# Low parts of the weights kept from the first half, and a selection operand shared by the groups, in a hybrid convolution and state-space layer

## The chip, the cores and the metric

The kernel runs on one core of a Trainium2 chip. The metric is the device time of one execution in microseconds. Three timed executions of the kernel before took 1994.49 to 1999.12 us, with a median of 1996.78 us. One more execution was recorded by the hardware profiler, and all rows shown here come from that one. The engines are called TensorE (PE in the rows), VectorE (DVE), ScalarE (ACT), GpSimd (POOL) and SyncE (SP, which issues most of the DMAs).

## The reference

One layer over 1024 positions and 1024 channels in float32, cut to its core:

```python
h = layer_norm(x, ln_in_g, ln_in_b)
u = h @ w_in[l]     # GLU | ssm z | ssm x,B,C | ssm dt | gate_a | gate_b
y_a = conformer_branch(u_glu, ...)  # GLU, 31-tap causal conv, LN, silu, @ w_conv_out
y_b = ssd_branch(z, xbc, dt_raw, ...)  # 4-tap conv, chunked SSD, group RMS norm, @ w_ssm_out
mix = (sigmoid(gate_a) * y_a + sigmoid(gate_b) * y_b) @ w_o[l]
h = layer_norm(DN_ALPHA * h + mix, ln1_g[l], ln1_b[l])
h = layer_norm(DN_ALPHA * h + conv_ffn(h, ...), ln2_g[l], ln2_b[l])
```

The SSD part has 32 heads of 64 channels in 4 groups of 8 heads, a state of 128, and chunks of 128 positions. Within a chunk, with a the decay rates of the chunk's positions:

```python
a_cs = jnp.cumsum(a, axis=-1)
seg = a_cs[..., :, None] - a_cs[..., None, :]
decay = jnp.where(causal, jnp.exp(jnp.where(causal, seg, 0.0)), 0.0)
cb = jnp.einsum("bclgn,bcsgn->bcgls", cc, bc)
y_diag = jnp.einsum("bcgrls,bcsgrp->bclgrp", cb[:, :, :, None] * decay, xs)
```

A scan over the chunks carries the state from one to the next.

## The kernel before

**Halves.** The 1024 positions are worked on as two halves of 512 (hh = 0 and 1 in the names, so `w_gt0_7` belongs to the first and `w_gt1_7` to the second). Each half goes through the input layer norm, `mixers`, `combine` and `out_proj`; the FFN follows for both. The projection weights of the mixers, the combination and the output are fetched from DRAM again in the second half.

**Weights.** Every product of float32 operands is made of three matmuls (`mm3`, L187 to L189) over a high and a low part. `weights` (L158) loads a tile of 128 x 1024 (512 KB) on SP into one of three staging buffers `st`, ScalarE casts it to the high part in `w[:, 0]` (L163), and VectorE subtracts that from `st` to give the low part in `w[:, 1]` (L164). There are three `w` buffers as well. `project` runs 24 matmuls for one tile, each with 512 columns. In the rest of the text these 512-column matmuls are called filler matmuls where they stand between the small products of the SSD part.

**Mixers.** For each of four groups: columns of the input projection and the four-tap convolution (`conv4`, L429), the GLU (L451, L452), the SSD chunks (`ssd_group`), z's gates (`z_gate`, L492) and the 31-tap convolution on VectorE (`conv31`, L474), whose result is stored to `c_scr` (L483). In a chunk, x and B are transposed (L520, L523), C and B are multiplied (L524) and masked to `cbm` (L546), and GpSimd forms `au` (L526), 8 copies of the decay selection `seg_mv`, one for each head of the group. Two matmuls (L535) of `seg_st` with `au` give the segment sums, which relu and exp turn into `m` (L543, L544). `xs` and `xsd` (L548, L553) are x times the step sizes; `bt` (L557) is B transposed, copied by ScalarE. L563 reads the state, L567 makes the chunk's contribution to it from `bt` and `xsd`, and L569 or L571 and L574 update it on VectorE. L577 gives y.

**Group norm.** The squares of a group's four tiles are added up on GpSimd (L602). `normed`, which runs later, sums them over the channels (L607), takes root and reciprocal (L612, L613), writes them to `r_scr` (L615), reads them back to all partitions into `ss` (L616), scales the tiles (L619) and splits them into `yT` (L203, L204).

**Combine.** Gate projections `gb`, the second half of the SSD output projection `sp` (which reads `yT` of the groups 2 and 3) and `co`, the convolution's output projection. In between stands the layer norm of the convolution: its eight tiles come back from `c_scr` (L696), GpSimd adds them up (L703, L705), and a matmul gives the mean (L707). That part has the scheduling priority `tc.high_priority(offset=900)`.

**Order.** The order of instructions on each engine isn't written by hand: a scheduler places them by a simulated timeline and by priorities, `offset=4000` for weights, and `offset=-1500` for the 31-tap convolution. Each engine then works through its list in order, and SP's list of DMAs too.

## Time and profile before

| | |
|---|---|
| median of three timed executions | 1996.78 us (1994.49 to 1999.12) |
| profiled execution, own time | 1997.45 us |
| its span, first to last instruction | 1995.7 us |
| granted TensorE clock, mean | 0.997 |
| VectorE, 31-tap convolution (L474) | 480 instructions, 385.2 us busy |
| GpSimd, `au` (L526) | 32 instructions, 79.8 us busy |
| GpSimd, squares (L602) | 24 instructions, 41.1 us busy |
| read and written in DRAM | 229.44 MB and 50.09 MB |

Busy shares say how much of the span an engine worked. A row of waits names an engine and a line that stood still, what it stood still for, and how long. A row of the timeline begins with the start and the duration in us; behind it, in brackets, stands how long the engine was idle before. A row of a line gives minimum, median and maximum of its durations in ns. A row of the DMA table gives the queue, the size and the median time from issue to landing in us.

### The profile page before, as it was taken

The numbers are of one execution on the slowest core, as the hardware profiler recorded it, in microseconds if no ns is written. First come the engines' busy times: TensorE is split into PE (matmuls) and PEld (weight loads), VectorE is DVE, ScalarE is ACT, GpSimd is POOL, SyncE is SP. The second block draws the span as 40 slices with busy tenths as digits, with TensorE's granted clock in tenths as the row PEclk, the third lists the DMA queues.
The fourth block names the chain that finished last, engine by engine and source line by source line (L and its number), as shares of the span: only waits on it lengthen the run. The fifth ranks groups of instructions, "written<-read, shape, count | busy, mean of one in ns | idle before, by whom it ended". The sixth has DMA issues, their size and how long they took to land.

```text
span 1995.7 us, 24843 instructions
## 1 busy us (share of the span) xinstructions
PE 1947.5 (98%) x9240; PEld 1592.9 (80%) x9240; DVE 1701.1 (85%) x2230; ACT 1052.9 (53%) x1483; POOL 237.4 (12%) x201
## 2 busy tenths in 40 slices
PE   7999999999999999999999999999999999999998
PEld 6887777877788887788777878887878888888886
DVE  7899999989565879999999967578998888778768
ACT  5566767454453266667654646256554544553442
POOL 1112121101400001111210132001000000011000
PEclk9999999999999999999999999999999999999999
DMA  6324232523544642324243354476443232268573
GB/s 218 111 65 121 73 117 79 164 81 115 175 127 155 240 140 77 102 84 117 80 132 116 100 185 127 132 279 241 170 148 116 101 113 104 102 215 272 181 248 111
DMA packets 99241, 281.15 MB, mean 141 GB/s; under 512 B 11728, under 2 KB 11760, under 8 KB 99120
## 3 DMA queue, kind: packets, MB, share of 16 engines
q1 hardware_dynamic: 87840, 244.68, 36.9%
q0 software_dynamic: 8976, 30.69, 5.1%
q10 hardware_dynamic: 2304, 4.20, 0.6%
q8 instruction: 72, 1.18, 0.2%
q14 instruction: 49, 0.40, 0.1%
HBM read 229.44 MB, written 50.09 MB: 140 GB/s over the span
## 4 chain that ended last, share of the span: by engine, by line
PE 64%; DVE 27%; issue 5%; DMA 2%; ACT 1%; POOL 1%; SPq 0%; DVEq 0%; POOLq 0%; ACTq 0%
PE acc L189 16%; PE acc L187 16%; PE acc L188 16%; DVE c L474 11%; PE sm L187 3%; PE sm L189 3%; PE sm L188 3%; DVE xbc L429 2%; DVE w_c L164 1%; PE acc L411 1%; DVE w_z L164 1%; DMA ss<-r_scr 1%; DVE m L558 1%; DVE xbc L619 1%; POOL mean L705 1%
## 5 line engine op out<-in xcount | busy, mean ns | idle before, releaser
L474 DVE SCALAR_TENSOR_TENSOR c<-v,pc,c 128x512 f32<-128x512 f32 x480 | 385.2, 832 | 5.5 <-ACT c L463 4.3
L187 PE MATMUL acc<-hT,w_c 128*128 128x512 f32 x352 | 141.6, 402 | 0.0
L189 PE MATMUL acc<-hT,w_c 128*128 128x512 f32 x352 | 138.5, 394 | 0.0
L188 PE MATMUL acc<-hT,w_c 128*128 128x512 f32 x352 | 137.9, 392 | 0.0
L526 POOL TENSOR_TENSOR au<-seg_mv,head_of 128x1024 fp32r<-128x1024 f32 x32 | 79.8, 2494 | 374.0 <-PE sm L535 373.9
L429 DVE SCALAR_TENSOR_TENSOR xbc<-u,pc,xbc 128x512 f32<-128x512 f32 x144 | 112.3, 794 | 0.5 <-ACT xbc L427 0.4
L987 DVE SCALAR_TENSOR_TENSOR fo<-u,pc,fo 128x1024 f32<-128x1024 f32 x88 | 111.4, 1286 | 0.4 <-ACT fo L983 0.4
L187 PE MATMUL acc<-h1s,w_s 128*128 128x512 f32 x264 | 103.5, 392 | 2.3 <-ACT u L971 2.3
L188 PE MATMUL acc<-hT,w_z 128*128 128x512 f32 x256 | 103.7, 405 | 0.0
L189 PE MATMUL acc<-h1s,w_s 128*128 128x512 f32 x264 | 103.0, 390 | 0.0
L188 PE MATMUL acc<-h1s,w_s 128*128 128x512 f32 x264 | 102.7, 389 | 0.0
L187 PE MATMUL acc<-hT,w_z 128*128 128x512 f32 x256 | 101.7, 397 | 0.0
L189 PE MATMUL acc<-hT,w_z 128*128 128x512 f32 x256 | 101.6, 397 | 0.0
L1126 ACT CAST w_dn<-dr 128x1024 fp32r<-128x1024 f32 (+1 forms) x73 | 61.0, 843 | 69.8 <-DVE dr L1056 33.3
L1127 DVE TENSOR_TENSOR w_dn<-dr,w_dn 128x1024 fp32r<-128x1024 f32 (+1 forms) x73 | 70.1, 968 | 13.5 <-ACT w_dn L1126 13.2
L188 PEld LDWEIGHTS acc<-hT,w_c 128*128 128x128 f32 x352 | 66.1, 188 | 15.7 <-issue 2.4
L187 PEld LDWEIGHTS acc<-hT,w_c 128*128 128x128 f32 x352 | 66.2, 188 | 15.3 <-issue 2.4
L189 PEld LDWEIGHTS acc<-hT,w_c 128*128 128x128 f32 x352 | 66.1, 188 | 14.5 <-issue 0.8
L163 ACT CAST w_c<-st_c 128x1024 fp32r<-128x1024 f32 x48 | 50.2, 1045 | 51.6 <-PE acc L189 32.5
L187 PE MATMUL sm<-h1b,w_s 128*128 128x512 f32 x176 | 69.1, 393 | 0.0
L188 PE MATMUL sm<-h1b,w_s 128*128 128x512 f32 x176 | 69.0, 392 | 0.0
L189 PE MATMUL sm<-h1b,w_s 128*128 128x512 f32 x176 | 69.0, 392 | 0.0
(372 smaller groups left out, 5708.3 us busy)
## 6 DMA issues: line engine op xcount, KB each, us to landing
st_c<-wcol SPq DMA_DIRECT2D x50, 512.0 KB, 3.5
st_z<-wz SPq DMA_DIRECT2D x32, 512.0 KB, 3.4
st_wo<-wo SPq DMA_DIRECT2D x24, 512.0 KB, 4.1
ra<-wup SPq DMA_DIRECT2D x22, 512.0 KB, 3.5
rb<-wup SPq DMA_DIRECT2D x22, 512.0 KB, 3.5
t_scr<-fo POOLq DMA_DIRECT2D x22, 512.0 KB, 3.4
dr<-t_scr SPq DMA_DIRECT2D x44, 256.0 KB, 3.8
dr<-wdown SPq DMA_DIRECT2D x38, 256.0 KB, 4.5
```

The costliest lines, as they stand in the source:

```text
L163: A.copy(w[:, 0, :], st)
L164: (eng or V).tensor_tensor(out=w[:, 1, :], in0=st, in1=w[:, 0, :].bitcast(F32), op=ALU.subtract)
L187: TE.matmul(ps, wa(0), xa(0), start=start, stop=False, skip_group_check=more)
L188: TE.matmul(ps, wa(0), xa(1), start=False, stop=False, skip_group_check=more)
L189: TE.matmul(ps, wa(1), xa(0), start=False, stop=stop, skip_group_check=more)
L411: TE.matmul(ps[:, ts], w[:, i, k * P : (k + 1) * P], hT[:, j, k, ts], start=n == 0 and k == 0, stop=n == 2 and k == KD - 1,)
L429: V.scalar_tensor_tensor(out=o, in0=u[:, k : k + HALF], scalar=pc[:, wc + k : wc + k + 1], in1=o, op0=ALU.mult, op1=ALU.add,)
L474: V.scalar_tensor_tensor(out=accs[i], in0=v[:, k : k + HALF], scalar=pc[:, wc + k : wc + k + 1], in1=accs[i], op0=ALU.mult, op1=ALU.add,)
L526: G.tensor_tensor(out=au, in0=seg_mv[:, c, :].unsqueeze(1).to_broadcast([P, 8, P]), in1=head_of[:, g, :].unsqueeze(2).to_broadcast([P, 8, P]),
L987: V.scalar_tensor_tensor(out=o, in0=u[:, k : k + T], scalar=pc[:, wc + k : wc + k + 1], in1=o, op0=ALU.mult, op1=ALU.add,)
L1126: A.copy(w[:, 0, cs], src)
L1127: V.tensor_tensor(out=w[:, 1, cs], in0=src, in1=w[:, 0, cs].bitcast(F32), op=ALU.subtract)
```

## The change

**Low parts.** In the first half `weights` stores each tile's low part to DRAM after the subtraction (96 tiles, 512 KB each, on SP). In the second half the same tile's low part is loaded into `w[:, 1]` on SP, and the subtraction is left out. Names that begin with `wo` (the weights of `out_proj`) are excluded, so the renaming in the last hunk changes a name only.

**Selection operand.** `au` is formed with all heads' lanes (`head_all`) and no longer depends on the group: GpSimd forms it for group 0 and stores it (8 times), and for the groups 1 to 3 it is loaded back on GpSimd's queue (24 times, 512 KB). The group enters through the other operand: ScalarE multiplies `seg_st` by the group's lanes into `sg` (128 x 128).

**Smaller edits.** The copy to `bt` stands right behind B's transposition. The squares of a group are added on VectorE. z's projections and their activations go in pairs. The convolution's layer norm has the priority 300 in place of 900. Two small reductions at the start form the lanes.

```diff
@@ -1,3 +1,4 @@
+import re
 from contextlib import ExitStack
 
 import concourse.bass as bass
@@ -112,6 +113,12 @@
         axis=AX.X,
         op=ALU.add,
     )
+    lanes = statep.tile([P, 16], F32, name="lanes")
+    head_all, group_of = lanes[:, :8], lanes[:, 8:12]
+    V.tensor_reduce(
+        out=head_all, in_=head_of.rearrange("p g h -> p h g"), axis=AX.X, op=ALU.add
+    )
+    V.tensor_reduce(out=group_of, in_=head_of, axis=AX.X, op=ALU.add)
     kind = const.tile([P, 4], F32, name="kind")
     V.tensor_reduce(
         out=kind, in_=ident.rearrange("p (g k h) -> p k g h", k=4, h=8), axis=AX.XY, op=ALU.add
@@ -152,18 +159,34 @@
     c_scr = [dram.tile([8, P, HALF], F32, name=f"c_scr{i}") for i in range(2)]
     g_scr = [dram.tile([8, P, HALF], F32, name=f"g_scr{i}") for i in range(2)]
     e_scr = [dram.tile([P, HALF], F32, name=f"e_scr{i}") for i in range(2)]
+    au_scr = [
+        [dram.tile([P, 8 * P], F32R, name=f"au_scr{i}_{c}") for c in range(4)] for i in range(2)
+    ]
     r_scr = [dram.tile([GROUPS, HALF], F32, name=f"r_scr{i}") for i in range(2)]
     y_scr = [dram.tile([8, P, HALF], F32, name=f"y_scr{i}") for i in range(2)]
 
+    low_scr = {}
+
     def weights(src, name, pl=None, eng=None, bufs=None):
+        half = re.match(r"([a-z]+)([012])_(.*)$", name)
+        if name.startswith("wo"):
+            half = None
+        key = half and (half.group(1), half.group(3))
         with tc.high_priority(offset=4000):
             st = wst.tile([P, D], F32, tag="st", name=f"st_{name}")
             SY.dma_start(st, src)
             w = (pl or wsp).tile([P, 2, D], F32R, tag="w", bufs=bufs, name=f"w_{name}")
+            if half and half.group(2) != "0" and key in low_scr:
+                SY.dma_start(w[:, 1, :].bitcast(F32), low_scr[key])
+                A.copy(w[:, 0, :], st)
+                return w
             A.copy(w[:, 0, :], st)
             (eng or V).tensor_tensor(
                 out=w[:, 1, :], in0=st, in1=w[:, 0, :].bitcast(F32), op=ALU.subtract
             )
+        if half and half.group(2) == "0":
+            low_scr[key] = dram.tile([P, D], F32, name=f"low_{name}")
+            SY.dma_start(low_scr[key], w[:, 1, :].bitcast(F32))
         return w
 
     def weights_side_by_side(src, name):
@@ -485,12 +508,14 @@
     def z_gate(pl, hh, hT, g):
 
         zs = []
-        for i in range(4):
-            ps = bank(1)
-            project(ps, weights(wz[4 * g + i], f"z{hh}_{g}_{i}"), hT)
-            z = pl.tile([P, HALF], F32, tag="zs", bufs=5, name=f"zs{hh}_{g}_{i}")
-            A.activation(out=z, in_=ps, func=AF.Silu)
-            zs.append(z)
+        for i in range(0, 4, 2):
+            pss = [bank(1) for _ in range(2)]
+            for k, ps in enumerate(pss):
+                project(ps, weights(wz[4 * g + i + k], f"z{hh}_{g}_{i + k}"), hT)
+            for k, ps in enumerate(pss):
+                z = pl.tile([P, HALF], F32, tag="zs", bufs=5, name=f"zs{hh}_{g}_{i + k}")
+                A.activation(out=z, in_=ps, func=AF.Silu)
+                zs.append(z)
         return zs
 
     def ssd_group(pl, hh, g, xT, BT, CT, gate):
@@ -521,20 +546,28 @@
             pb = bank(0)
             if not last:
                 TE.transpose(pb[:, :P], BT[:, cs], ident)
+                bt = pl.tile([P, P], F32, tag="bt", name=f"bt{nm}")
+                A.copy(bt, pb[:, :P])
             TE.matmul(pb[:, P : 2 * P], BT[:, cs], CT[:, cs], start=True, stop=True)
             au = pl.tile([P, 8, P], F32R, tag="au", name=f"au{nm}")
-            G.tensor_tensor(
-                out=au,
-                in0=seg_mv[:, c, :].unsqueeze(1).to_broadcast([P, 8, P]),
-                in1=head_of[:, g, :].unsqueeze(2).to_broadcast([P, 8, P]),
-                op=ALU.mult,
-            )
+            if g == 0:
+                G.tensor_tensor(
+                    out=au,
+                    in0=seg_mv[:, c, :].unsqueeze(1).to_broadcast([P, 8, P]),
+                    in1=head_all.unsqueeze(2).to_broadcast([P, 8, P]),
+                    op=ALU.mult,
+                )
+                G.dma_start(au_scr[hh][c], au.rearrange("p h l -> p (h l)"))
+            else:
+                G.dma_start(au.rearrange("p h l -> p (h l)"), au_scr[hh][c])
+            sg = pl.tile([P, P], F32R, tag="sg", name=f"sg{nm}")
+            A.mul(sg, seg_st[:, c, :].bitcast(F32), group_of[:, g : g + 1])
             m = pl.tile([P, 8, P], F32, tag="m", name=f"m{nm}")
             for q in range(2):
                 pg = bank(0)
                 TE.matmul(
                     pg,
-                    seg_st[:, c, :],
+                    sg,
                     au[:, 4 * q : 4 * q + 4, :].rearrange("p h l -> p (h l)"),
                     start=True,
                     stop=True,
@@ -553,8 +586,6 @@
                 V.tensor_tensor(
                     out=heads(xsd), in0=heads(px), in1=per_head(dts[1][:, c, h8]), op=ALU.mult
                 )
-                bt = pl.tile([P, P], F32, tag="bt", name=f"bt{nm}")
-                A.copy(bt, pb[:, :P])
             V.tensor_tensor(out=m, in0=m, in1=cbm.unsqueeze(1).to_broadcast([P, 8, P]), op=ALU.mult)
             if not first:
                 po = bank(0)
@@ -599,7 +630,7 @@
             else:
                 sq = pl.tile([P, HALF], F32, tag="yo", bufs=2, name=f"sq{hh}_{g}_{i}")
                 A.activation(out=sq, in_=y, func=AF.Square)
-                G.tensor_add(ss, ss, sq)
+                V.tensor_add(ss, ss, sq)
 
         def normed(yT):
             pm = bank(0)
@@ -689,7 +720,7 @@
                 V.tensor_add(m, ya, ps)
                 V.tensor_mul(m, m, gb)
                 mb.append(m)
-            with tc.high_priority(offset=900):
+            with tc.high_priority(offset=300):
                 cs = []
                 for i in range(8):
                     c = pl.tile([P, HALF], F32, tag=f"c{i}", name=f"cc{hh}_{i}")
@@ -779,7 +810,7 @@
             pss = {(t, q): bank(1) for t in ts for q in range(2)}
             for kp in range(4):
                 for q in range(2):
-                    w = weights(wo[q, kp], f"wo1_{pair}_{q}_{kp}")
+                    w = weights(wo[q, kp], f"wo{pair + 1}_{q}_{kp}")
                     for t in ts:
                         for k in range(2):
                             mm3(
```

**How rows move.** Rows show line, operation, output <- input and shape; the line numbers of the changed kernel are some 16 to 31 higher. The first place is TensorE in the first half, group 0, at the start of the third chunk (`sm36`: transposed x, `sm37`: B transposed and C with B, `sm38`: the segment sums). Before:

```order
L520 MATMUL sm36_938<-ident_75,xbc0_0_585 128x128
L520 MATMUL sm36_938<-ident_75,xbc0_1_625 128x128
L520 MATMUL sm36_938<-ident_75,xbc0_2_665 128x128
L520 MATMUL sm36_938<-ident_75,xbc0_3_705 128x128
L523 MATMUL sm37_943<-ident_75,xbc0_16_535 128x128
L524 MATMUL sm37_943<-xbc0_20_545,xbc0_16_535 128x128
L535 MATMUL sm38_949<-au0_0_2_946,seg_st_137 128x512
```

After:

```order
L545 MATMUL sm36_975<-ident_75,xbc0_0_602 128x128
L545 MATMUL sm36_975<-ident_75,xbc0_1_644 128x128
L545 MATMUL sm36_975<-ident_75,xbc0_2_686 128x128
L545 MATMUL sm36_975<-ident_75,xbc0_3_728 128x128
L548 MATMUL sm37_980<-ident_75,xbc0_16_550 128x128
L568 MATMUL sm38_991<-au0_0_2_985,sg0_0_2_988 128x512
```

The product of C and B (L524, now L551) no longer follows the transposition directly; it stands 20 filler matmuls further on. The filler matmuls between the state's product of the chunk before (L567, now L598) and these rows were 17 and are 40; in the second half they are 32.

The second place is VectorE in the first half, where the first chunk of group 1 meets the norm of group 0 (`xbc0_0` to `xbc0_3` and `ss0_0` belong to the norm, `xs0_1_0`, `xsd0_1_0` and `cbm0_1_0` to the chunk, `c0_1` and later are taps). Before:

```order
L548 TENSOR_TENSOR xs0_1_0_1666<-sm65_1645,dtv_133 128x512
L553 TENSOR_TENSOR xsd0_1_0_1668<-sm65_1645,wds_134 128x512
L474 SCALAR_TENSOR_TENSOR c0_2_1977<-v0_2_1570,pc_114,c0_2_1977 128x512
L546 TENSOR_TENSOR cbm0_1_0_1664<-sm66_1650,upper_92 128x128
L164 TENSOR_TENSOR w_z0_1_2_1897<-st_z0_1_2_1895,w_z0_1_2_1897 128x1024
L452 TENSOR_TENSOR v0_3_1636<-acc63_1576,sig0_3_1637 128x512
L204 TENSOR_TENSOR yT0_0_1487<-xbc0_0_585,yT0_0_1487 128x512
L204 TENSOR_TENSOR yT0_0_1487<-xbc0_1_625,yT0_0_1487 128x512
L474 SCALAR_TENSOR_TENSOR c0_1_1183<-v0_1_840,pc_114,c0_1_1183 128x512
```

After, the rows of the chunk:

```order
L497 SCALAR_TENSOR_TENSOR c0_2_2064<-v0_2_1637,pc_117,c0_2_2064 128x512
L497 SCALAR_TENSOR_TENSOR c0_3_2066<-v0_3_1707,pc_117,c0_3_2066 128x512
L579 TENSOR_TENSOR cbm0_1_0_1739<-sm66_1721,upper_92 128x128
L497 SCALAR_TENSOR_TENSOR c0_2_2064<-v0_2_1637,pc_117,c0_2_2064 128x512
L497 SCALAR_TENSOR_TENSOR c0_3_2066<-v0_3_1707,pc_117,c0_3_2066 128x512
```

and 11 rows on, after `cbm` and with more taps between, those of the norm:

```order
L497 SCALAR_TENSOR_TENSOR c0_3_2066<-v0_3_1707,pc_117,c0_3_2066 128x512
L600 COPY state1_133<-sm69_1746 128x512
L497 SCALAR_TENSOR_TENSOR c0_2_2064<-v0_2_1637,pc_117,c0_2_2064 128x512
L227 TENSOR_TENSOR yT0_0_1550<-xbc0_0_602,yT0_0_1550 128x512
L184 TENSOR_TENSOR w_c0_38_2175<-st_c0_38_2173,w_c0_38_2175 128x1024
```

The scaling of the norm stood ahead of the chunk's `xs`, `xsd` and `cbm`; now it stands behind them and behind `m`. In the second half, groups 1 and 2, `xs` and `xsd` stand behind the scaling.

The third place is SP in the second half, in the gates of the convolution branch (`st_` are staged weights, `c_scr` and `g_scr` stores of results, `w_...<-low_...` the loads of low parts). Before:

```order
L161 DMA st_gt1_7_9322<-wcol 128x1024
L661 DMA g_scr1_196<-gt1_2_9186 128x512
L161 DMA st_gb1_0_9360<-wcol 128x1024
L661 DMA g_scr1_196<-gt1_3_9219 128x512
L483 DMA c_scr1_194<-c1_6_9002 128x512
L161 DMA st_gb1_1_9392<-wcol 128x1024
L661 DMA g_scr1_196<-gt1_4_9252 128x512
L161 DMA st_sp1_0_9426<-wssm 128x1024
```

After:

```order
L177 DMA st_gt1_6_9564<-wcol 128x1024
L692 DMA g_scr1_199<-gt1_0_9373 128x512
L506 DMA c_scr1_197<-c1_6_9277 128x512
L180 DMA w_gt1_4_9500<-low_gt0_4_4241 128x1024
L177 DMA st_gt1_7_9597<-wcol 128x1024
L692 DMA g_scr1_199<-gt1_1_9406 128x512
L180 DMA w_gt1_5_9533<-low_gt0_5_4276 128x1024
L177 DMA st_gb1_0_9635<-wcol 128x1024
L692 DMA g_scr1_199<-gt1_2_9461 128x512
L506 DMA c_scr1_197<-c1_7_9279 128x512
L180 DMA w_gt1_6_9566<-low_gt0_6_4311 128x1024
```

Between the loads of whole weights now stand the loads of low parts, some of them right behind the store of a convolution's result.

Two more places, in words. TensorE's matmul of the last group norm in the first half (L607, now L638) stood behind the fifth matmul of `gt0_7`, and now stands behind all of `gb0_0`; up to the first matmul that reads channels of group 3 in `sp0_0` there were 79 filler matmuls and are 60. The matmul of the convolution's mean (L707, now L738) stood 129 filler matmuls behind that of the group norm in the first half and 132 in the second, and now 151 and 145. In the FFN no engine's order differs.

## The prediction

> **What bounds the kernel now.** I read the page first, then the waits of TensorE, then single lines, the timeline and the table of DMA issues.
>
> ```profile
> span 1995.7 us, 24843 instructions
> PE 1947.5 (98%) x9240; PEld 1592.9 (80%) x9240; DVE 1701.1 (85%) x2230; ACT 1052.9 (53%) x1483; POOL 237.4 (12%) x201
> PE 64%; DVE 27%; issue 5%; DMA 2%; ACT 1%; POOL 1%; SPq 0%; DVEq 0%; POOLq 0%; ACTq 0%
> ```
>
> TensorE is busy for 1947.5 of 1995.7 us, and the change takes no projection from it. VectorE at 85% looks like the next limit, and the chain that ended last gives it 27%. But that is a share of an average: VectorE can only cost time where TensorE stands still for it. So the list of TensorE's waits is what can be won:
>
> ```profile
> PE sm L213 <- DVE x L264: 13.0, 2, 11.8
> PE sm L535 <- DVE state L574: 5.3, 5, 1.7
> PE sm L707 <- POOL mean L705: 4.6, 2, 3.5
> PE sm L567 <- ACT bt L557: 4.1, 3, 1.8
> PE acc L189 <- DVE w_ga L164: 2.4, 1, 2.4
> ...
> PE sm L535 <- DVE state L569: 1.6, 1, 1.6
> PE sm L563 <- DVE xsd L553: 1.5, 1, 1.5
> PE acc L189 <- DVE w_so L164: 1.3, 1, 1.3
> ```
>
> The columns are the total in us, how many times, and the longest. The first row is the head and the first hand-over of the layer norm, which nothing in the change touches. The other seven touch what the change edits: 5.3 + 4.6 + 4.1 + 2.4 + 1.6 + 1.5 + 1.3 = **20.8 us**, 1.0% of the span. That is the most that can be gained, however much VectorE work goes.
>
> How fast TensorE goes through its filler work gives the unit for every cover below:
>
> ```profile
> 599.68 0.39 PE L188 MATMUL acc<-sT,w_co 128*128 128x512 f32 x1
> ...
> 601.72 0.39 PE L188 MATMUL acc<-sT,w_co 128*128 128x512 f32 x1
> ```
>
> Nine starts lie between these two: (601.72 - 599.68) / 9 = 0.227 us for each 512-column matmul, and 24 of them, one weight tile, take 5.44 us.
>
> **The low parts.** In the second half 96 subtractions leave VectorE, and 96 stores of 512 KB (first half) and 96 loads (second half) join SP's queue.
>
> ```profile
> L164 DVE TENSOR_TENSOR w_c<-st_c,w_c x46: 1207/1214/1226, 33.9 to 997.8; 128x1024 fp32r<-128x1024 f32 x46
> SPq L161 <- DVE w_c L164: 274.3, 42, 10.6
> st_c<-wcol SPq DMA_DIRECT2D x50, 512.0 KB, 3.5
> ```
>
> 96 x 1.214 = 117 us of VectorE work goes. On TensorE's path lie only the waits for w_ga and w_so, 2.4 + 1.3 us, both in the second half, where the producer they wait for no longer exists. Next in line is the low load: it may start when TensorE has left the buffer, three tiles back, so it has two tiles, 10.9 us, and needs 3.5 us at rest. SP itself has slack: it stands in long waits for w_c as it is, so 192 more issues don't add to the end. The stores of the first half wait for the same subtraction that frees the next weight's staging buffer, so they hold nothing up that didn't wait there already.
>
> How bad can a load be? The busiest stretch shows it, the end of the output projection just before the first low loads:
>
> ```profile
> 640.00:680.00 40.00, 39.15 (x189) 32.59 (x188) 32.34 (x48) 12.49 (x20) 0.00 (x0) 1.00 0.79 302
> st_wo<-wo SPq DMA_DIRECT2D x2, 512.0 KB, 9.9
> 1160.00:1200.00 40.00, 38.94 (x172) 30.76 (x171) 24.69 (x27) 15.19 (x21) 14.77 (x11) 1.00 0.62 199
> ```
>
> The last two columns of a window are the DMA share and GB/s; the middle row is the landing in 650 to 680. At 302 GB/s a load took 9.9 us, 1.0 us inside the cover. The steady second half will move 1 MB per 5.44 us, 193 GB/s, besides its small transfers, near the last window:
>
> ```profile
> st_gb<-wcol SPq DMA_DIRECT2D x4, 512.0 KB, 4.0
> ```
>
> That is st_gb's landing in 1160 to 1200, so 6.9 us of the cover stay there. I take 0.5 us for the first loads of the half and for one behind the burst of cc loads; bounds 0 and 3.
>
> **The SSD chunks** (group masks, bt copied early, squares summed on VectorE).
>
> ```profile
> L474 DVE SCALAR_TENSOR_TENSOR c<-v,pc,c x480: 641/741/2391, 76.2 to 1163.9; 128x512 f32<-128x512 f32 x160
> L526 POOL TENSOR_TENSOR au<-seg_mv,head_of x32: 1896/2110/7598, 69.0 to 1118.4; 128x1024 fp32r<-128x1024 f32 x32
> L602 POOL TENSOR_TENSOR ss<-ss,sq x24: 1293/1626/2683, 160.0 to 1160.4; 128x512 f32<-128x512 f32 x24
> 299.62 3.81 POOL L526 TENSOR_TENSOR au<-seg_mv,head_of 128x1024 fp32r<-128x1024 f32 x1 [10.89 <-PE sm L535]
> 301.60 2.38 DVE L474 SCALAR_TENSOR_TENSOR c<-v,pc,c 128x512 f32<-128x512 f32 x1
> ```
>
> A convolution tap of 0.741 us took 2.38 us beside a POOL au product. 24 of the 32 products and all 24 ss additions leave POOL. Against that VectorE gets 24 additions, 24 x 0.74 = 18 us. All of this is VectorE time, not end time, until it moves one of the seven waits.
>
> [...]
>
> What counts is the place. The state waits (5.3 + 1.6 us) arise where the next chunk's seg matmul follows the state product by 17 matmuls, 17 x 0.227 = 3.9 us. In the changed order there are 40 (9.1 us) in the first chunks of the first half and 32 (7.3 us) in the second. The update behind it is one copy, or a multiplication and an addition, of about 0.68 us each on VectorE:
>
> ```profile
> L574 DVE TENSOR_TENSOR state<-state,sm x24: 669/676/680, 108.6 to 1127.5; 128x512 f32<-128x512 f32 x24
> L557 ACT COPY bt<-sm x28: 242/266/274, 87.3 to 1118.7; 128x128 f32<-128x128 f32 x28
>   DVE cbm L546: 24.1, 14
> ```
>
> Even behind two or three instructions of VectorE's queue that fits into 7.3 us, so I take the whole 6.9 us. The bt wait (4.1 us): ACT's bt copy was held by cbm (last row), which stood behind the group scaling L619 on VectorE, which waits for a DMA. Now bt waits for the transpose alone, and CB's matmul, which must now wait for bt, stands 20 matmuls further on, 4.5 us for a copy of 0.27 us. I take 4.1 us.
>
> The xsd wait (1.5 us, at 1087 us) goes with its place, but in the second half xs and xsd of groups 1 and 2 stand behind the scaling again. Each can have a wait like that row: 0 to 3.0 us; I take 1.5.
>
> The 24 au reloads on POOL's queue are compared with the nearest POOL loads:
>
> ```profile
> t_scr<-fo POOLq DMA_DIRECT2D x22, 512.0 KB, 3.4
> ys<-e_scr POOLq DMA_DIRECT2D x16, 512.0 KB, 6.7
> ```
>
> From the seg matmuls that free an au tile's buffer to those that read the next lie at least 32 filler matmuls (7.3 us) and the chunk's small products, some 9 us, so either landing is hidden: bounds 0 and, for the slower row with 2 us of queue, also 0.
>
> **Norm and combine.** The mean matmul was late by 4.6 us in two places. It stood 129 matmuls after the group norm's matmul in the first half, now 151, and 132 and now 145 in the second. 22 x 0.227 = 5.0 us against a wait of 3.5, and 13 x 0.227 = 3.0 against 1.1: both go. That the conv norm then ends some 5 us later costs nothing: its last split was at 1237.9 in the second half, and its reader waits for the sp products. But the last group norm of the first half has less cover:
>
> ```profile
> 494.99 1.04 PE L607 MATMUL sm<-ss,pick 128*4 128x128 f32 x8
> 496.82 0.36 ACT L612 ACTIVATE rr<-sm,eps 4x128 f32<-4x128 f32 x1
> 500.13 0.93 DVE L613 RECIPROCAL rr<-rr 4x128 f32<-4x128 f32 x1
> 509.15 2.74 DVE L619 SCALAR_TENSOR_TENSOR xbc<-xbc,nskip,ss 128x512 f32<-128x512 f32 x4 [6.22 <-DMA ss<-r_scr]
> 511.81 2.49 DVE L204 TENSOR_TENSOR yT<-xbc,yT 128x512 fp32r<-128x512 f32 x4
> 529.04 1.65 PE L707 MATMUL sm<-mean,mean_w 128*128 128x512 f32 x2 [3.52 <-POOL mean L705]
> 1196.86 1.13 PE L707 MATMUL sm<-mean,mean_w 128*128 128x512 f32 x2 [1.06 <-POOL mean L705]
> ```
>
> From 494.99 the first split is done at about 511.81 + 2.49/4 = 512.4, 17.4 us later. Before, 79 matmuls (17.9 us) stood between; now gb0_1, half of sp0_0 and gb0_2 do, 60 matmuls, 13.6 us and about 0.9 for the norm's own matmuls: 14.5. **New wait** 17.4 - 14.5 = 2.9 us; if VectorE takes the reciprocal at once (it lay from 497.18 to 500.13) there is none. I take 2.4, nearer to the row. Pairing z's activations moves the first gate of a pair back by one weight tile, 5.44 us, and no row of the list waits for a gate: 0. The 32 masked copies sg on ACT are of bt's size, 32 x 0.27 = 9 us on an engine that is 53% busy, and stand ahead of the seg matmuls by the transposes: 0, or one ACT instruction of 1.05 us at a bad place. The FFN's rows keep their order on every engine: 0.
>
> **Sum.** -20.8 + 2.4 (yT) + 1.5 (xsd) + 0.5 (low loads) = -16.4. The profiled execution took 1997.45 us, so 1981.05; it lay 0.67 above the median 1996.78, so I say **1981 us**, -0.8%.
>
> **Rivals.**
>
> *Slower: a low load behind a waiting transfer.* SP works in order. In the second half low loads stand straight behind 8 stores of c, which wait for the last tap, and behind 8 loads of yb, which wait for a buffer.
>
> ```profile
> SPq L483 <- DVE c L474: 39.3, 16, 8.4
> SPq L685 <- DVE mb L689: 33.1, 12, 6.2
> ```
>
> A load behind the longest wait lands 8.4 + 4.0 = 12.4 us after its buffer came free, 1.5 us over the cover of 10.9. If that held behind all 16, it costs 16 x 1.5 = 24 us: 1981 + 24 = 2005. It decides from a wait of 10.9 - 4.0 = 6.9 us on. Against it: the mean waits are 39.3/16 = 2.5 and 33.1/12 = 2.8 us, and taps end sooner when VectorE has 117 us less. 0.10.
>
> *No change: the waits move.* TensorE meets the same chains at other places: the seven waits come back at nearly their size, 20.8 - 3 = 18 us: 1995. For it: the order is rebuilt everywhere, and the 2.4 and 1.5 above already show it. 0.16.
>
> [...]
>
> *It does less than it says.* The names of the output weights begin with wo and are excluded, so 24 subtractions stay; they never held TensorE, so the price is 0 and no case of its own.
>
> *All waits go and none comes:* 1976.65. 0.10.
>
> **Chances and range.** Forecast 0.60 (1977 to 1990), none left 0.10, moved 0.16, behind stores 0.10, starved 0.04. This measurement can tell about 0.2%, 4 us. Faster takes the forecast and the case without waits and some of the moved one: 0.72; same 0.15; slower 0.13. The range leaves out the two slow cases: 1974 to 1998.
>
> **What would show it.** Right: the seven rows gone from TensorE's waits, POOL under 150 us, VectorE about 120 us lower and mostly after 690 us, and one wait for yT near 510 us of 1 to 3 us. Wrong: rows of TensorE waiting for w_ DMAs in the second half (behind stores), for au, or new waits for xsd or state that together pass 10 us.

## The result and the profile after

| | before | changed |
|---|---|---|
| timed executions, median | 1997.95 us (1994.49 to 2000.15, 4 runs) | 1975.60 us (1972.36 to 1978.27, 4 runs) |
| profiled execution, own time | 1997.45 us | 1978.27 us |
| span | 1995.7 us | 1976.6 us |

The ratio is 0.9889, with a 95% interval of 0.9865 to 0.9913: 1.1% faster. The sum of the prediction was 1981.05 us for the profiled execution, which took 1978.27; the forecast of 1981 us lay 5.4 above the median.

First the page of the changed kernel: busy times, and what went to and from DRAM.

```profile
span 1976.6 us, 25102 instructions
PE 1940.3 (98%) x9240; PEld 1590.6 (80%) x9240; DVE 1554.8 (79%) x2160; ACT 1073.7 (54%) x1523; POOL 147.3 (7%) x185
HBM read 292.35 MB, written 104.61 MB: 201 GB/s over the span
```

VectorE's busy time fell by 146 us (1701.1 to 1554.8) and GpSimd's by 90, and the span by 19. The DRAM traffic rose by 117 MB, from 279.5 to 397. Now TensorE's waits, with the columns as before:

```profile
PE sm L236 <- DVE x L287: 15.0, 3, 12.5
PE acc L210 <- ACT u L1002: 2.3, 2, 1.2
PE acc L210 <- ACT yT L226: 2.2, 1, 2.2
PE acc L211 <- DVE yT L227: 1.4, 1, 1.4
PE sm L598 <- DVE xsd L586: 1.3, 1, 1.3
PE acc L210 <- ACT w_wo L183: 1.1, 1, 1.1
...
PE acc L212 <- DMA w_sp<-low_sp: 0.7, 1, 0.7
PE sm L551 <- ACT bt L550: 0.5, 1, 0.5
```

All seven rows that could be won are gone, except for the xsd row, which stands at another place. The new ones sum to 2.2 + 1.4 + 1.3 + 1.1 + 0.7 + 0.5 = 7.2 us. The list thus falls by 20.8 - 7.2 = 13.6, less 2.0 that the first row grew. The span fell by 19.1, so 7.5 us of it don't show in these rows; the paragraph on the clock further down accounts for some of them.

### The profile page after: what moved, and what is told of

The parts are those of the page before. It is cut to its first block, busy times and chain, and to the rows that moved or that the text cites. A ratio compares the mean times of both kernels' runs of the same rounds, so it can differ in the third digit from the quotient of the medians.

```text
span 1976.6 us, 25102 instructions
## 1 busy us (share of the span) xinstructions
PE 1940.3 (98%) x9240; PEld 1590.6 (80%) x9240; DVE 1554.8 (79%) x2160; ACT 1073.7 (54%) x1523; POOL 147.3 (7%) x185
## 4 chain that ended last, share of the span: by engine, by line
PE 42%; DVE 4%; issue 3%; DMA 3%; ACT 1%; POOL 0%; SPq 0%; DVEq 0%; POOLq 0%; ACTq 0%
PE acc L210 10%; PE acc L212 10%; PE acc L211 10%; PE sm L210 3%; PE sm L212 3%; PE sm L211 3%; DVE w_dn L1158 1%; DMA st_wo<-wo 1%; DMA do<-wdown 1%; DMA ss<-r_scr 1%; DVE rows L284 1%; DVE rows L287 0%; POOL mean L736 0%; DMA dr<-wdown 0%; DVE st_f L251 0%
## 5 line engine op out<-in xcount | busy, mean ns | idle before, releaser
L497 DVE SCALAR_TENSOR_TENSOR c<-v,pc,c 128x512 f32<-128x512 f32 x480 | 349.4, 755 | 8.9 <-ACT c L486 6.9
L452 DVE SCALAR_TENSOR_TENSOR xbc<-u,pc,xbc 128x512 f32<-128x512 f32 x144 | 107.2, 754 | 11.3 <-ACT xbc L450 10.9
L211 PEld LDWEIGHTS acc<-hT,w_c 128*128 128x128 f32 x352 | 66.1, 188 | 15.1 <-issue 1.9
L210 PE MATMUL acc<-h1b,w_ue 128*128 128x512 f32 x168 | 65.6, 390 | 0.9 <-ACT first L940 0.9
L211 PE MATMUL acc<-h1b,w_ue 128*128 128x512 f32 x168 | 65.4, 389 | 0.0
```

The lines of the kernel that those rows point to most:

```text
L210: TE.matmul(ps, wa(0), xa(0), start=start, stop=False, skip_group_check=more)
L211: TE.matmul(ps, wa(0), xa(1), start=False, stop=False, skip_group_check=more)
L452: V.scalar_tensor_tensor(out=o, in0=u[:, k : k + HALF], scalar=pc[:, wc + k : wc + k + 1], in1=o, op0=ALU.mult, op1=ALU.add,)
L497: V.scalar_tensor_tensor(out=accs[i], in0=v[:, k : k + HALF], scalar=pc[:, wc + k : wc + k + 1], in1=accs[i], op0=ALU.mult, op1=ALU.add,)
```

## The experiments

Two theories stood at the start. P: what counts is how many filler matmuls stand between the small products, which the placement of the edits decides. D: what counts is VectorE's load, so the 117 us of subtraction that went carry the gain. Each kernel was timed beside the kernel before, and its ratio is to that. The first four ran on one chip and the later ones on another, so between these two sets the ratios are compared, or the spans of the profiles. "Without low parts" means the kernel of the third run below, which became the measure of the later ones. The first four:

**The changed kernel again** (no edit).

> The changed kernel again, as the measure for the others on this chip. Both theories: 22 us faster than before (1975 to 1978 us), TensorE's waits as in its first profile: one for yT in the first half (2.2 + 1.4 us), one for xsd (1.3), none for state or mean.

1979.12 us, ratio 0.9905 (0.9887 to 0.9923), span 1977.1; 1 us above what was expected. The yT row again (2.7 and 1.4 us), the xsd row with 0.5.

**Only the low parts**, in the kernel before.

```diff
 (the kernel before)
+        if half and half.group(2) == "0":
+            low_scr[key] = dram.tile([P, D], F32, name=f"low_{name}")
+            SY.dma_start(low_scr[key], w[:, 1, :].bitcast(F32))
...
+            if half and half.group(2) != "0" and key in low_scr:
+                SY.dma_start(w[:, 1, :].bitcast(F32), low_scr[key])
+                A.copy(w[:, 0, :], st)
+                return w
```

> The kernel before with the low parts alone stored and loaded (no shared selection operand, bt late, squares on GpSimd, priority 900). Theory P, places: the waits for state, bt and xsd depend on how many filler matmuls stand between a chunk's rows, and these stay as tight as before (17 and 10 in the first half, 23 to 28 in the second), so the first half keeps its state and bt waits (4.5 + 4.1 us); w_ga and w_so (3.7) go, and of the mean's 4.6 most goes (141 and 139 matmuls behind the norm). Gain 7 to 10 us, 1988 to 1991. Theory D, VectorE's load: the 117 us taken off VectorE carry the gain, so most of the 22 us is there, 1976 to 1982.

2009.81 us, ratio 1.0057 (1.0042 to 1.0073): **slower** than before, against both theories. From its page and its waits:

```profile
PE 1955.4 (97%) x9240; PEld 1598.4 (80%) x9240; DVE 1589.7 (79%) x2134; ACT 1052.2 (52%) x1482; POOL 232.8 (12%) x201
PE sm L581 <- ACT bt L571: 13.0, 6, 3.9
PE sm L721 <- POOL mean L719: 3.0, 1, 3.0
PE sm L577 <- ACT m L557: 3.0, 2, 1.9
PE sm L549 <- DVE state L588: 2.8, 2, 2.1
```

VectorE has 111 us less to do than before, and TensorE waits more: bt 13.0 us in place of 4.1. The gain that D forecast didn't come, and the low parts are no small gain but a loss. The same edit adds the traffic of the stores and loads, so this run alone doesn't price VectorE's load.

**Everything but the low parts.**

```diff
 (the changed kernel)
-            if half and half.group(2) != "0" and key in low_scr:
-                SY.dma_start(w[:, 1, :].bitcast(F32), low_scr[key])
-                A.copy(w[:, 0, :], st)
-                return w
...
-        if half and half.group(2) == "0":
-            low_scr[key] = dram.tile([P, D], F32, name=f"low_{name}")
-            SY.dma_start(low_scr[key], w[:, 1, :].bitcast(F32))
```

> The changed kernel without the low parts (subtraction in both halves), all else as changed. P: the chunks keep their wide spacing (28 to 54 fillers), so state and bt waits stay away in both halves; waits for w_ tiles by VectorE's subtraction come back in the second half (3 to 5 us), and part of the mean's (139 and 133 matmuls, 1 to 3 us). Gain 13 to 17 us, 1980 to 1984. D: VectorE is as full as before in the second half, the gain is under 8 us, above 1989, with state waits in the second half.

1969.52 us, ratio 0.9854 (0.9837 to 0.9871): 9.6 us faster than the changed kernel on the same chip, and the best ratio of the study. Both expectations were too slow (P 1980 to 1984, D above 1989). These are its busy times and all its waits of TensorE over 0.5 us:

```profile
PE 1938.8 (99%) x9240; PEld 1591.1 (81%) x9240; DVE 1666.8 (85%) x2256; ACT 1070.7 (54%) x1521; POOL 153.3 (8%) x185
PE sm L223 <- DVE x L274: 14.7, 3, 12.3
PE acc L197 <- ACT u L989: 2.3, 2, 1.2
PE acc L197 <- ACT first L927: 0.9, 1, 0.9
PE acc L197 <- DVE r L783: 0.9, 1, 0.9
```

VectorE is as full as before in its share (85%), and no wait over 0.5 us in the mixers or the combination is left, not even one for the w_ tiles that the subtraction held up before.

**bt late**, in the changed kernel: the copy stands behind `xsd` again.

```diff
-                bt = pl.tile([P, P], F32, tag="bt", name=f"bt{nm}")
-                A.copy(bt, pb[:, :P])
             TE.matmul(pb[:, P : 2 * P], BT[:, cs], CT[:, cs], start=True, stop=True)
...
+            if not last:
+                bt = pl.tile([P, P], F32, tag="bt", name=f"bt{nm}")
+                A.copy(bt, pb[:, :P])
             V.tensor_tensor(out=m, in0=m, in1=cbm.unsqueeze(1).to_broadcast([P, 8, P]), op=ALU.mult)
```

> The changed kernel with only the copy to bt put back behind xsd, in the program's order. The scheduler then places 12 to 30 fillers between the state's product and the next chunk in most chunks. P: state and bt waits come back, 4 to 9 us, so 1980 to 1985. D: VectorE's load is the changed kernel's, no wait comes back, within 2 us of the changed kernel.

1979.81 us, ratio 0.9910 (0.9894 to 0.9927): the same as the changed kernel. P's price didn't come. Its profile, of the longest of the six executions (1985.02), has a wait of 3.5 us for the mean and 1.9 for ys, and no state row; bt's has 0.3.

So a third theory was needed for the loss by the low parts. In the first half the order of TensorE around the last group norm is the same, row by row, with and without low parts (gb0_0, the norm's matmul, gb0_1, half of sp0_0, gb0_2). The chain that follows differs. With low parts, in the timeline of the changed kernel:

```profile
491.83 1.04 PE L638 MATMUL sm<-ss,pick 128*4 128x128 f32 x8
494.69 0.94 DVE L644 RECIPROCAL rr<-rr 4x128 f32<-4x128 f32 x1 [0.45 <-ACT rr L643]
495.92 0.51 POOL L646 DMA_DIRECT2D r_scr<-rr  x1 [50.34 <-DVE rr L644]
500.68 0.57 POOL L647 DMA_DIRECT2D ss<-r_scr  x1 [4.25 <-DMA r_scr<-rr]
507.45 2.74 DVE L650 SCALAR_TENSOR_TENSOR xbc<-xbc,nskip,ss 128x512 f32<-128x512 f32 x4 [6.55 <-DMA ss<-r_scr]
```

And without:

```profile
493.18 1.04 PE L625 MATMUL sm<-ss,pick 128*4 128x128 f32 x8
496.04 0.94 DVE L631 RECIPROCAL rr<-rr 4x128 f32<-4x128 f32 x1 [0.45 <-ACT rr L630]
497.27 0.51 POOL L633 DMA_DIRECT2D r_scr<-rr  x1 [50.34 <-DVE rr L631]
499.79 0.57 POOL L634 DMA_DIRECT2D ss<-r_scr  x1 [2.01 <-DMA r_scr<-rr]
503.23 2.74 DVE L637 SCALAR_TENSOR_TENSOR xbc<-xbc,nskip,ss 128x512 f32<-128x512 f32 x4 [0.97 <-DMA ss<-r_scr]
```

Up to the issue of r_scr both take 4.09 us. Then the store and the load take 4.76 + 6.77 = 11.5 us with low parts and 2.52 + 3.44 = 6.0 without. Theory T: the traffic of the low parts lengthens the two small DMAs of every group norm, and what waits for the norm waits for that. Its rival Q: the low loads block SP's queue while they wait for TensorE's buffers.

The kernel with the low parts alone points the same way. VectorE's scaling of the norm stood there longer for `ss` (the first row is of the kernel before, the second of that with the low parts alone):

```profile
DVE xbc L619 <- DMA ss<-r_scr: 20.9, 5, 6.2
DVE xbc L633 <- DMA ss<-r_scr: 49.3, 7, 10.0
```

The longest of its bt waits, 3.85 us, ends at 191.37 us. The scaling had begun at 185.74 after 4.37 us of standing for `ss`, `cbm` followed at 190.25 and bt at 191.06. Before, the same matmul waited 0.73 us. The order of this kernel isn't wholly that of the kernel before, so its 12 us aren't shown to come from T alone.

**Stores in the first half, never loaded.** The second half subtracts.

```diff
 (the changed kernel)
-            if half and half.group(2) != "0" and key in low_scr:
-                SY.dma_start(w[:, 1, :].bitcast(F32), low_scr[key])
-                A.copy(w[:, 0, :], st)
-                return w
```

> The changed kernel with the low parts stored in the first half but never loaded; the second half subtracts. TensorE's order is the changed kernel's in the first half and that of the kernel without low parts in the second. Theory T, traffic: the stores lengthen the small DMAs of the norm in the first half (r_scr 4.3 to 4.8 us to its landing against 2.0 to 2.5, ss 6.8 against 3.4), so the yT wait of 3.5 to 4 us with the clock's drop behind it is back, and the second half has no waits: 1973 to 1976 us, 4 to 6 above the kernel without low parts (1969.5). Theory Q, the queue: the cost comes from loads that wait on SP for TensorE's buffers, so stores alone are within 2 us of 1969.5 and no yT wait shows.

1973.95 us, ratio 0.9881 (0.9867 to 0.9895), span 1972.0, 3.9 above that of the kernel without low parts. By the ratios it is some 5 us; the two intervals just touch. The yT rows are back:

```profile
PE acc L206 <- ACT yT L222: 1.7, 1, 1.7
PE acc L207 <- DVE yT L223: 1.4, 1, 1.4
```

Both kernels have 60 filler matmuls between the last norm's matmul and the first that reads its channels. From the issue of r_scr's store to the scaling it takes 11.0 us here and 6.0 without low parts. T holds for the first half; Q can't explain it, for nothing is loaded.

**Extra traffic in the second half** by copies from DRAM to DRAM.

```diff
 (without low parts)
+            if re.match(r"(?!wo)[a-z]+1_", name):
+                again = dram.tile([P, D // 2], F32, name=f"again_{name}")
+                SY.dma_start(again, src[:, : D // 2])
```

> The changed kernel without low parts, and in the second half each weight tile's load is followed on SP by a copy of half the tile from DRAM to DRAM (256 KB read, 256 KB written, nobody waits for it): about the traffic of the low loads without their waits. Leaves nothing out. T: ss and r_scr land 1 to 3 us later in the second half, where covers are larger, so 0 to 4 us above 1969.5, with waits for xsd or yT. Q: within 1 us of 1969.5, no wait.

2008.52 us, ratio 1.0049 (1.0036 to 1.0062), but the experiment missed its place. The copies depend on nothing, and all 96 were issued in the first 115 us, where 327 GB/s were moved in the first 100 us; there the profile has waits of 5.1 us for m, 4.5 for w_ga and 4.0 for w_c. In the window 700 to 1340 us the traffic was 141 GB/s against 144 without low parts, so nothing was added there, and the only wait there was 1.1 us for w_wo. It tells nothing of T in the second half.

**Stores in the second half**, none in the first, and no load: the repaired version of it.

```diff
 (the kernel with stores only)
-        if half and half.group(2) == "0":
+        if half and half.group(2) == "1":
```

> The kernel without low parts, with 96 stores of 512 KB in the second half (each low part after its subtraction, never loaded), none in the first. Adds traffic to the second half alone, with no wait for TensorE's buffers. Theory T, traffic: the small loads of ss land 1 us later in the second half as in the changed kernel (4.9 against 4.0 us), and one or two waits for xsd or yT of 1 to 3 us come: 1 to 4 us above the kernel without low parts. Rival, order: the changed kernel's waits of the second half (xsd, w_sp, bt, 2 to 3.6 us) come from its other order and from loads behind TensorE, so the stores cost under 1 us.

1979.89 us, ratio 0.9903 (0.9887 to 0.9920), by the ratios 10 us above the kernel without low parts, where T expected 1 to 4. The five executions fall into two groups, 1973.17 and 1974.18 us and three of 1979.89 to 1980.83, so the loss isn't the same each time. The profile is of one of the three (1980.21). Its waits:

```profile
PE sm L564 <- DVE state L601: 2.4, 2, 2.1
...
PE acc L206 <- ACT yT L222: 1.6, 1, 1.6
PE acc L207 <- DVE yT L223: 1.4, 1, 1.4
```

All of these are in the second half now (the yT wait ends at 1162.9 us), where the kernel without low parts has none. The landing times of r_scr's stores, min/median/max, tell the halves apart. Without low parts, first half:

```profile
DMA to landing us min/median/max: 1.6/1.6/2.0
```

With stores in the first half, first half:

```profile
DMA to landing us min/median/max: 2.9/3.2/4.3
```

The same kernel in the second half, where it stores nothing:

```profile
DMA to landing us min/median/max: 1.6/2.0/2.4
```

And with stores in the second half, second half:

```profile
DMA to landing us min/median/max: 2.9/3.3/4.0
```

Wherever the stores run, r_scr takes 3.2 or 3.3 us in place of 1.6 or 2.0, and ss goes from 4.2 to 4.9 in the first half and from 3.7 to 5.9 in the second (medians).

In the second half the stores moved the order as well: between the last norm's matmul and the first that reads its channels stand 47 filler matmuls, and 54 without stores. The kernel with au on GpSimd, further below, has 46 there, stores no low parts and reloads no au. Its r_scr issue and scaling stand first, those of the kernel with stores in the second half behind them:

```profile
1148.63 0.54 POOL L629 DMA_DIRECT2D r_scr<-rr  x1 [47.93 <-DVE rr L627]
1154.43 2.74 DVE L633 SCALAR_TENSOR_TENSOR xbc<-xbc,nskip,ss 128x512 f32<-128x512 f32 x4 [2.61 <-DMA ss<-r_scr]
1152.10 0.52 POOL L642 DMA_DIRECT2D r_scr<-rr  x1 [51.14 <-DVE rr L640]
1161.46 2.74 DVE L646 SCALAR_TENSOR_TENSOR xbc<-xbc,nskip,ss 128x512 f32<-128x512 f32 x4 [5.94 <-DMA ss<-r_scr]
```

That is 5.8 us without a wait for yT, and 9.4 us with one. So the DMAs make this wait, and not the shorter cover alone. T is shown for the stores, by the wait for yT in both halves; how much the new order adds to the 10 us isn't separated.

No run tells by what the stores lengthen the small DMAs.

**Which of the other edits carry the gain?** First bt alone, in the kernel before.

```diff
             if not last:
                 TE.transpose(pb[:, :P], BT[:, cs], ident)
+                bt = pl.tile([P, P], F32, tag="bt", name=f"bt{nm}")
+                A.copy(bt, pb[:, :P])
```

> The kernel before with only the copy to bt moved behind the transposition. The spacing becomes nearly the changed kernel's (30, 40, 43 in the first group, 24 to 49 elsewhere). P: state and bt waits (5.3 + 1.6 + 4.1 us, with clock drops) go, the mean's stays (128 and 134 matmuls), w_ waits may stay: 9 to 14 us faster than before, 1983 to 1988. Rival (VectorE's and GpSimd's load): under 5 us faster, since au products and squares on GpSimd still stretch VectorE.

1990.51 us, ratio 0.9963 (0.9950 to 0.9976), some 7 us faster than before where P expected 9 to 14. The bt row is gone and the state rows fell from 6.9 to 1.1 us, as P says, but the chunk now waits elsewhere:

```profile
PE sm L567 <- DVE xsd L555: 9.3, 5, 3.5
...
PE sm L707 <- POOL mean L705: 2.2, 2, 1.5
PE sm L577 <- DVE m L558: 2.0, 1, 2.0
```

The wait moved from bt to xsd, the other operand of the same matmul. This edit alone brings 0.37% of the 1.46% that the kernel without low parts gained, a quarter. The other way round, four of the edits were taken out of the kernel without low parts, one at a time. **bt late there:**

> The kernel without low parts with the copy to bt put back behind xsd. The scheduler then leaves 22, 22 and 30 fillers in groups 0 and 3 of the first half in place of 30, 40 and 35. Theory P (places): waits for bt, state or m of 2 to 6 us come back, 1972 to 1977. Rival: VectorE has the slack of the other edits, no wait, within 1.5 us of 1969.5.

1972.62 us, ratio 0.9868 (0.9853 to 0.9882), span 1971.2, 3.1 more. No bt, state or xsd row, but the mean's with 2.5 us and w_wo's with 1.1. The intervals overlap; a small loss at most.

**au on GpSimd for all groups**, the same without reloads:

```diff
-            if g == 0:
-                G.tensor_tensor(
+            G.tensor_tensor(
...
-            else:
-                G.dma_start(au.rearrange("p h l -> p (h l)"), au_scr[hh][c])
```

> The kernel without low parts, with au formed on GpSimd for all groups again (32 products, no reload). 24 products beside VectorE take it some 24 x 1.6 = 39 us. Theory P, places: the chunks keep their spacing, TensorE meets no new wait over 1 us, within 2 us of the kernel without low parts (0.985 of before). Theory D, VectorE's load: state or xsd waits of 3 to 8 us come back.

**The squares on GpSimd** (`G.tensor_add` in place of `V.tensor_add`):

> The kernel without low parts, with the squares added on GpSimd again. The scheduler then sets the norms 3 to 46 fillers earlier and leaves 25 to 33 fillers in some chunks of groups 1 and 2. P: xsd waits as in the kernel before with only bt moved (9.3 us in 5 places) come back in part: 2 to 8 us, 0.986 to 0.990. Rival: all spacings stay above 24, no wait, within 1.5 us.

**Priority 900** for the convolution's layer norm in place of 300:

> The kernel without low parts, with the convolution's layer norm at priority 900 again: its mean matmul stands 133 and 127 fillers behind the norm's in place of 139 and 133, nothing else moves much. By the distances 6 x 0.227 = 1.4 us is lost at each: a wait for the mean of 0 to 3 us in all, and if one passes some 2 us, the clock's drop behind it adds 1.7. 0.985 to 0.988. Rival: the mean is ready earlier anyway, no wait.

1969.09, 1968.76 and 1968.81 us, ratios 0.9860, 0.9860 and 0.9858, with intervals between 0.9845 and 0.9876: no difference from the kernel without low parts (0.9854) in any of the three. With au on GpSimd a tap takes 781 ns in the mean, against 757 without low parts and 832 before:

```profile
L484 DVE SCALAR_TENSOR_TENSOR c<-v,pc,c 128x512 f32<-128x512 f32 x480 | 362.8, 781 | 3.0 <-ACT c L473 2.2
```

VectorE has 21 us more to do (1687.8 against 1666.8) and TensorE doesn't notice. P had expected xsd waits of 2 to 8 us with the squares on GpSimd, and 0 to 3 us for the mean with priority 900. In none of the three did a wait over 0.3 us appear in the mixers or the norm of the convolution. So no single one of these three is needed for the gain, and the early bt is worth some 3 us there at the median, while bt alone brings a quarter of it. Which two or three together remove the xsd waits is open; the pairing of z and the selection operand `sg` were not run by themselves.

## Why the prediction was right, and where it wasn't

**What bounds the kernel:** right. TensorE's waits held what could be won, the rows went, and 146 us off VectorE moved the span by 19. VectorE's load isn't what sets the time: without low parts it is back at 85% and the ratio is the best, and with au on GpSimd it has 21 us more to do in the same time.

**The most that can be gained:** wrong. The prediction put it at 20.8 us. The kernel without low parts took 28.3 us less than the kernel before on its chip (1969.52 against 1997.77) and 27.6 less in its span. A sum of the rows of waits isn't a bound, since a wait can cost more than its row: two of the seven rows' waits had 1.7 us at half clock behind them, as the paragraph on the clock shows. Not all of the difference is accounted for.

**The size of the gain:** right by luck. The prediction's terms are -3.2 for the low parts and -13.2 for all else. On one chip the runs gave +9.6 for the low parts and -28.3 for all else. Two errors of 12.8 and 15.1 us cancelled, and left -18.7 there where -16.4 was forecast.

**The low parts:** wrong in sign. The step that failed is "The stores of the first half wait for the same subtraction that frees the next weight's staging buffer, so they hold nothing up that didn't wait there already", with "I take 0.5 us" for the loads. Queue and cover were weighed for the large transfers themselves, which did stay inside (one low load was late, by 0.7 us), and the small DMAs on a chain of dependences were left at their old landings. The low parts were put at -3.7 + 0.5 = -3.2 us; with and without them the changed kernel differs by 9.6 us the other way (1979.12 against 1969.52), and alone they cost 12 us. Of the 9.6, the stores of the first half alone cost 4 to 5, with the yT wait shown to return. The rest lies in the second half. The changed kernel's waits there for xsd, w_sp and bt are part of it; its wait for w_wo is not, for that stands without low parts too (1.1 us with bt late). There the low loads came together with another order, and loads alone were not run, so what makes up the rest is open.

**The waits for w_ga and w_so** went as forecast, but not for the reason given: they are gone as well where the subtraction is still there, without low parts and with bt alone.

**The new wait for yT:** forecast 2.4, measured 3.6 in the same place, and the size was luck. The cover of 14.5 us was right, and fewer matmuls are part of the cause. But the prediction filled the time with a queued reciprocal, and that ran at once: it began 2.9 us after the norm's matmul (494.69 - 491.83) in place of 5.1 (500.13 - 494.99), which by the prediction would mean no wait. In its place the time from the reciprocal's end to the scaling grew from 8.1 to 11.8 us, by the two DMAs. With the same 60 matmuls and short DMAs there is no wait. The bound of 0 was the value that the other edits alone give.

**The xsd wait** in the second half: forecast 1.5, measured 1.3 (0.5 in the second profile), in group 1 behind the scaling of the norm (xs begins at 932.61, after L650 at 929.29), as described.

**State, bt, mean:** gone as forecast (bt 0.5 left). That wide spacing and an early bt remove the waits for state and bt is shown by the kernel with bt alone. But with the other edits in, a late bt costs some 3 us, so the 6.9 + 4.1 us aren't the price of this one edit: several of the edits remove the same waits. For the mean the distance that the priority gives was not the reason, or not alone: at priority 900 and without low parts its matmul stands 133 and 127 filler matmuls behind the norm's, near the 129 and 132 before, and doesn't wait.

**The rivals:** loads behind SP's waiting transfers cost one wait of 0.7 us, and the au reloads none (4.9 us at the median, no wait). "The waits move" held for bt alone, where xsd took over.

**A term that was missing: the clock.** The sum took a wait for its own length. The windows of 2 us around the yT wait of the changed kernel show more; the third column from the right is the granted clock:

```profile
508.00:510.00 2.00, 0.49 (x1) 0.19 (x1) 2.00 (x4) 1.67 (x3) 0.00 (x0) 1.00 0.30 117
510.00:512.00 2.00, 1.15 (x4) 0.91 (x5) 2.00 (x5) 1.94 (x4) 0.00 (x0) 0.82 0.00 0
512.00:514.00 2.00, 2.00 (x6) 1.59 (x5) 1.74 (x2) 1.99 (x3) 0.00 (x0) 0.50 0.21 45
514.00:516.00 2.00, 2.00 (x9) 1.58 (x8) 0.69 (x1) 1.43 (x3) 0.02 (x1) 0.82 1.07 302
```

After the wait the clock stands at half for about 3.4 us (in windows of 0.5 us it is 0.80 from 511.0, 0.50 in all six from 511.5 to 514.5, and 0.79 in the next): (0.18 + 0.50 + 0.18) x 2 = 1.7 us lost on top. Before, two waits had such a tail, that for the mean (3.5 us; 0.87, 0.50 and 0.77 in the three windows of 2 us from 528) and that for w_ga (2.4 us; 0.82, 0.50 and 0.83 from 832). In the changed kernel one has: of the windows of 40 us up to 1960, that from 480 to 520 has 0.96 and all others 1.00. One tail fewer is 1.7 of the 2.8 us by which the sum missed the profiled execution, and 1.7 of the 7.5 us that the rows of waits don't show. A row also counts a wait short. It begins at the end of the matmul before, 0.39 us after its start, where by the prediction's two rows the next could start after 0.227. By that, 0.16 us for each of 14 waits before and 6 after make another 1.3 us, an estimate. The other 4.5 us stay open.

## What to carry to other kernels

Look for the waits of the engine that bounds, not for the busiest engine beside it: here 146 us off VectorE came with 19 us, and giving it the subtractions back, with less traffic, brought another 10, while moving one copy of 0.27 us behind its producer bought 7. When a change adds large transfers, ask first which small DMAs lie on a chain of dependences at the same time, and price those at the landing that they have in the busiest stretch. And test the parts of a change one by one: this one is 1.1% faster, and 1.5% with the low parts taken out again.

## What the runs showed of the hardware

The granted clock can fall after a wait of TensorE of some 2 us, and the length of the wait alone doesn't decide it. Waits of 2.4 us (w_ga, before), of 2.1 us (state, with stores in the second half) and of 1.9 us (xsd, with bt alone, at 419 us) were followed by a stretch at a lower clock: 0.50 from 834 to 836 us, 0.96 over 840 to 880 and 0.96 over 400 to 440. One of 2.2 us (xsd, with bt alone, at 309 us) was not, with 1.00 over 280 to 320, nor were those of up to 1.8 us before (bt and state), with 1.00 over 280 to 320 and over 400 to 440. What else decides it, the runs don't show. These are the windows of 40 us with the state wait and with the two yT waits of the kernel with stores in the second half:

```profile
840.00:880.00 40.00, 37.95 (x193) 30.18 (x192) 37.02 (x54) 26.61 (x41) 1.69 (x4) 0.96 0.56 179
1160.00:1200.00 40.00, 36.98 (x148) 29.38 (x148) 24.10 (x31) 17.85 (x25) 18.14 (x13) 0.91 0.80 257
```

0.96 is a loss of 0.04 x 40 = 1.6 us, 0.91 one of 3.6, more than the yT waits of 1.6 + 1.4 us themselves. With the low parts alone eight windows of 40 us show such a loss, by 13 us together.

Small DMAs slowed down well below the highest traffic seen. Over the first 700 us the kernel without low parts moved 148 GB/s and the changed one 224, while 302 were moved from 640 to 680 us before the change; at 224 r_scr's store already took 3.1 us at the median of the first half, against 1.6. The mean traffic doesn't settle a single landing: in the kernel before, at 131 GB/s over the same stretch, two of the first half's four stores landed in 1.5 and 1.6 us and two in 3.1 and 3.2.
